# Two stacked decoder layers on one core: another order for loading the expert weights

## The chip, the cores and the metric

The kernel runs on one core of a Trainium2 chip. The metric is the device time of one execution in microseconds (us). A core has a matrix engine (TensorE, PE in the profile), a vector engine (VectorE, DVE), an activation engine (ScalarE, ACT) and a sync engine (SyncE, SP) which here issues nearly all DMA transfers. Each engine works through its own instructions in their order and waits on semaphores of the others.

## The reference

Two layers over 256 tokens of width 1024. Each has a norm, four mixers and their gates, an output projection, then a feed-forward part: dense in the first layer, and in the second the best two of eight experts for each token. The change touches only that expert part:

```python
def _moe(h, router_w, wg, wu, wd):
    logits = t @ router_w                       # (256, 8)
    vals, idx = lax.top_k(logits, 2); w = softmax(vals)
    gate = sum(one_hot(idx, 8) * w[..., None], axis=1)
    for e in range(8):
        y = y + gate[:, e:e+1] * ((silu(t @ wg[e]) * (t @ wu[e])) @ wd[e])
```

`wg[e]` and `wu[e]` are 1024 x 3584, `wd[e]` is 3584 x 1024, all float32: 44 MB for each expert, 352 MB in all, read once.

## The kernel before

The first 857 us of the execution are the first layer and the mixers of the second. After that comes `experts()`, in `run()`.

**Whole experts and pairs.** The experts are sorted by how many tokens they have. The four largest are *whole*: up to 128 tokens each. The four smallest make two *pairs*: two experts side by side, 64 tokens each. The hidden width 3584 is cut into 7 chunks of 512. A *step* is one chunk of a whole expert or of a pair. Of 42 steps 28 are whole and 14 are of pairs; `PAIRS` puts one pair step after every second whole step, and the last ones close together.

**Pieces.** The weights come in pieces of 1 MB (128 x 2048 float32). A whole step uses six: two for the gate product (`gps`), two for the up product (`ups`), and then two for the down product (`yps`) of the whole step before. A pair step uses twelve: first four for the down product of the pair step before (`yps`), then four for `gps`, four for `ups`. In each of a pair's products calls (L1308) two pieces, one for each expert, are used together. `pieces()` lists all 336 pieces in the order of use.

**Split pieces and raw pieces.** A whole expert's piece lands in a `raw` tile and is then split: ACT copies its high part into `wh` (L164), DVE subtracts that and leaves the low part in `wl` (L171), and PE makes three products of it (L196 to L198). Its raw tile is free once DVE is done. There are three `wh` and three `wl` buffers. A pair's piece lands in a `rawn` tile and PE reads it there (L1308); its tile is free once PE has used it.

**The ring.** `Stream.begin()` takes raw tiles in turn out of nine (`rawp` has 4, `rawx` 5). SP issues a transfer once the tile nine places earlier in the order of loading is free. All issues stand in one queue of SP. `Stream.get()` (called in `products()`) hands out the next piece, and before that writes the loading and splitting of pieces into the program until two beyond this one are there. PE, ACT and DVE keep the order in which the program is written.

**Other work in the steps.** Small jobs wait in a list `units`; `tick()` runs one between products. Before an expert's or a pair's first step its tokens are gathered (`gather()`: tile `dms` on DVE, then eight groups of products L1218 into `gaps`, copied out by ACT and DVE); after its last step the result is scattered (L1341). Gate products end in L1371 (`act`, on ACT). `turned()` transposes `act` of a step for its down product: PE L243, then ACT L1325 for a pair (`aT`), ACT L214 and DVE L215 for a whole expert (`ah`, `al`); it stands after the gate products of a whole step, for the pair and then for the whole step before.

Of the kernel before, what the change touches and what calls it, by code (L numbers as in the profile page):

```python
# [25 lines left out]
KD = D // P  # L26
# [10 lines left out]
NB = 4  # L37
# [27 lines left out]
def trunk(ctx: ExitStack, tc: tile.TileContext, x, pos, invf, rows, cols, wst, w_a, w_kvf, w_gate, w_br,  # L65
          w_out, f_g, f_u, f_d, router, e_g, e_u, e_d, gfin, out):
    nc = tc.nc
# [89 lines left out]
    def load_hi(src, n=512, parts=1, pool=None):  # L157

        raw = (pool or rawp).tile([P, 4 * n], F32, tag="raw", name="raw")
        hi = whp.tile([P, 4 * n], F32R, tag="wh", name="wh")  # L160
        sls = [slice(4 * n * i // parts, 4 * n * (i + 1) // parts) for i in range(parts)]
        for sl in sls:
            nc.sync.dma_start(raw[:, sl], src[:, sl])
            nc.scalar.activation(hi[:, sl], raw[:, sl], AF.Copy)  # L164
        return raw, hi, sls, n

    def load_lo(raw, hi, sls, n):

        lo = whp.tile([P, 4 * n], F32R, tag="wl", name="wl")
        for sl in sls:  # L170
            nc.vector.tensor_sub(lo[:, sl], raw[:, sl], hi[:, sl].bitcast(F32))  # L171
        return hi.rearrange("p (k n) -> p k n", k=4), lo.rearrange("p (k n) -> p k n", k=4)
# [874 lines left out]
    def experts(l, mine):  # L1047
# [3 lines left out]
        with ExitStack() as c2:  # L1051
# [10 lines left out]
            class Stream:  # L1062

                def __init__(self, srcs, ahead=2, whole=False):
                    self.srcs, self.begun, self.ready, self.ahead = list(srcs), [], [], ahead
                    self.whole = whole

                def begin(self):  # L1070
                    (w, q, *rest), parts = self.srcs.pop(0)
                    if q and not places:
                        _, vals = nc.values_load_multi_w_load_instructions(
                            idx_i[0:1, 0:NE], engines=[E.SP], min_val=0, max_val=NE - 1)
                        places.extend(vals)
                    src = w[(places[q] if q else 0, *rest)]
                    pool = ([rawp] * 4 + rawx)[turn[0] % (4 + NX)]
                    turn[0] += 1
                    if q < NB or self.whole:
                        self.begun.append(load_hi(src, parts=parts, pool=pool))  # L1080
                    else:
                        raw = pool.tile([P, 4 * W], F32, tag="raw", name="rawn")
                        n = 4 * W // parts
                        for i in range(parts):
                            nc.sync.dma_start(raw[:, i * n:i * n + n], src[:, i * n:i * n + n])
                        self.begun.append(raw.rearrange("p (k n) -> p k n", k=4))

                def fill(self):
                    while (self.srcs or self.begun) and len(self.ready) <= self.ahead:
                        if not self.begun:  # L1090
                            self.begin()
                        b = self.begun.pop(0)
                        self.ready.append(load_lo(*b) if isinstance(b, tuple) else b)

                def get(self):
                    self.fill()
                    return self.ready.pop(0)

            gate, mx, e8 = small("gate", NT, NE), small("mx", 2, NT), small("e8", NT, NE)
            gts = small("gts", NT, NE, 2, dtype=F32R)  # L1100
# [55 lines left out]
            class Expert:  # L1156
# [2 lines left out]

                def __init__(self, *at, base=0):  # L1160
                    self.at, self.pair, self.base = at, len(at) > 1, base
                    self.y = [None, None]

            def pieces(steps):

# [8 lines left out]
            def run(steps, groups, stream, tagx):  # L1174


                with ExitStack() as c3:
                    wk = c3.enter_context(tc.tile_pool(name=f"xk{tagx}", bufs=2, reuse_waits="tile"))
                    units, late = [], []

                    def tick(n=1):

                        for _ in range(n):
                            if late:
                                late.pop(0)()
                            if units:
                                then = units.pop(0)()
                                if then:
                                    late.append(then)
# [18 lines left out]
                    def token_tiles(group):  # L1208
                        for x in group:
                            if x.pair:  # L1210
                                x.tok = wk.tile([P, KD, P], F32, tag="xs", name="xs")
                            else:
                                x.tok = wk.tile([P, KD, 2, P], F32R, tag="xb", name="xb")
# [7 lines left out]

                    def gather_out(group, ps, part, k2):
                        for i, x in enumerate(group):
                            ks, src = slice(2 * k2, 2 * k2 + 2), ps[:, :, i * P:(i + 1) * P]
                            if not x.pair:
                                nc.scalar.activation(x.tok[:, ks, part], src, AF.Copy)
                            elif part == 0:
                                nc.scalar.activation(x.tok[:, ks], src, AF.Copy)
                            else:
                                nc.vector.tensor_add(x.tok[:, ks], x.tok[:, ks], src)  # L1230
# [45 lines left out]
                    def gather_now(x, dm):  # L1276


                        token_tiles([x])
                        banks = [(4 * g, part, py.tile([P, 4, P], F32, tag="y", name="gaps0"))  # L1280
                                 for g in range(2) for part in range(2)]
                        for t in range(NT):
                            if t:
                                mine.slot(psm, t)
                            for k0, part, ps in banks:
                                for i in range(4):
                                    k = k0 + i
                                    nc.tensor.matmul(ps[:, i], mine.parts[t][part][:, k * P:(k + 1) * P], dm[:, t, 0],
                                                     start=not t and not i, stop=t == NT - 1 and i == 3)
                                if t:  # L1290
                                    dst = x.tok[:, k0:k0 + 4, part]
                                    if part:
                                        nc.vector.tensor_copy(dst, ps)
                                    else:
                                        nc.scalar.activation(dst, ps, AF.Copy)
# [87 lines left out]
                    def turned(pair):  # L1383
                        if prev[pair] and not lhs[pair]:
                            lhs[pair] = act_T(prev[pair][0], prev[pair][2])
# [7 lines left out]
                    for n, (x, c) in enumerate(steps):  # L1393
                        if n == 0:
                            if x.base:
                                gather([x])
                                tick(len(units) + 1)
                            else:
                                gather_now(x, mine.dm)
                        if x.pair:  # L1400
                            down_of(1)
                            prev[1] = x, c, gate_up(x)
                            continue

                        def meanwhile():
                            if not x.base:
                                if n == 0:
                                    in_places()
                                if n == 1:
                                    gates()  # L1410
                                if n in groups:
                                    gather(groups[n])
                                if n == 0:
                                    units.append(lambda x=x: back([x], mine.dm))
                            for pair in (1, 0):
                                turned(pair)
                        a = gate_up(x, meanwhile)
                        down_of(0)
                        prev[0] = x, c, a


                    nc.scalar.activation(frs[:, 0:1], epsc, AF.Sqrt)
# [4 lines left out]
                    x = steps[-1][0]  # L1427
# [33 lines left out]
            q = [Expert(i) for i in range(NB)]  # L1461
            p = [Expert(i, i + 1) for i in range(NB, NE, 2)]
            steps = [(x, c) for x in q for c in range(NFC)]
            for at, s in reversed(list(zip(PAIRS, [(x, c) for x in p for c in range(NFC)]))):
                steps.insert(at + 1, s)
            groups = {steps.index((x, c)): g for x, c, g in
                      ((q[0], 0, [p[0], q[1]]), (q[1], 3, [p[1], q[2]]), (q[2], 3, [q[3]]))}
            order = [(s, 1) for s in pieces(steps)]
            order[-6:] = [(s, 4) for s, _ in order[-6:]]
            stream = Stream(order[3:])  # L1470
            stream.ready, stream.begun = mine.first[:1], mine.first[1:]
            run(steps, groups, stream, "a")
            finish("a")
            with tc.If(nc.values_load(over_i[0:1, NE:NE + 1], min_val=0, max_val=1) > 0):
                for i in range(NE):
                    with tc.If(nc.values_load(over_i[0:1, i:i + 1], min_val=0, max_val=1) > 0):
                        x = Expert(i, base=P if i < NB else P // 2)
# [80 lines left out]
```

## Time and profile before

| what | value |
|---|---|
| runs | 1753.75, 1751.87, 1753.71 us; median 1753.71 |
| the profiled execution | 1754.09 us, of which the span from the first to the last instruction is 1752.4 us |
| busy share of the span | PE 95%, weight loads of PE 70%, DVE 60%, ACT 47% |
| mean granted clock of TensorE | 0.985 |
| moved by DMA | 497.69 MB, mean 284 GB/s |
| chain of waits | PE 47%, DMA 8%, ACT 4%, DVE 4% |

Busy PE is not PE at its peak: the ends of its pipelined matmuls are modelled. In the rows below a `windows` row gives a stretch in us from the span's start, its length, the busy time of PE, PEld, DVE, ACT and POOL with instruction counts, the granted clock, the DMA engines' busy share and GB/s. A `timeline` row gives start, duration, engine, line, operation, out<-in, count, and in brackets the idle time before it with what ended it. A row of the chain of waits gives start, duration, and what it was spent on. In the name of a row's operand `in_e_g`, `in_e_u` and `in_e_d` are the gate, up and down weights of the experts.

### The profile page before, as it was taken

To read this page: it belongs to the slowest core of one execution; us is meant where nothing else is said; L and a number is where in the kernel's file an instruction comes from. 1 tells how busy PE (TensorE), PEld (TensorE's weight loads), DVE (VectorE), ACT (ScalarE), POOL (GpSimd) and SP (SyncE) were. 2 spreads that over 40 slices of the span, in tenths; PEclk is the share of its full clock that TensorE was granted. 3 is DMA by queue.
4 is the path that set the end of the run, shared out by engine and by line. 5 is a ranking of instruction groups with operands and counts; after the bars stand their busy time and mean duration, and the time that the engine had idled before them with its cause. 6 is when DMAs were issued, how large, how long until landed. Compare 5 with 4: busy or idle time off the path is not lost.

```text
span 1752.4 us, 20308 instructions
## 1 busy us (share of the span) xinstructions
PE 1672.5 (95%) x7800; PEld 1225.4 (70%) x7800; DVE 1052.6 (60%) x1284; ACT 828.0 (47%) x878; POOL 12.5 (1%) x28
## 2 busy tenths in 40 slices
PE   8999999999999999999889999999999899999995
PEld 6888888888887888888776557556556655755552
DVE  6779976555545678976665437435545633754434
ACT  6655454544434656444465426434443533543333
POOL 1000000000000000000000000000000000000000
PEclk9999999999999999999899999999999999999998
DMA  7444444555554543446568999999999989999994
GB/s 269 169 145 145 169 173 162 207 180 190 190 182 154 197 145 123 170 176 257 221 231 361 408 421 421 421 392 386 422 415 420 417 344 418 420 421 420 420 419 162
DMA packets 74362, 497.69 MB, mean 284 GB/s; under 512 B 8368, under 2 KB 8416, under 8 KB 15888
## 3 DMA queue, kind: packets, MB, share of 16 engines
q1 hardware_dynamic: 73008, 492.93, 71.5%
q0 software_dynamic: 960, 2.85, 0.6%
q8 instruction: 63, 1.03, 0.2%
q10 hardware_dynamic: 288, 0.52, 0.1%
q14 instruction: 43, 0.35, 0.1%
HBM read 495.22 MB, written 1.05 MB: 283 GB/s over the span
## 4 chain that ended last, share of the span: by engine, by line
PE 47%; DMA 8%; ACT 4%; DVE 4%; issue 1%; SPq 0%; ACTq 0%; DVEq 0%
DMA raw<-in_e_g 6%; PE yps L1308 6%; PE gps L197 3%; PE yps L197 3%; PE yps L196 3%; PE yps L198 3%; PE zps L196 3%; PE gps L198 3%; PE zps L198 3%; PE zps L197 3%; PE gps L196 3%; PE ups L196 3%; PE ups L197 3%; ACT wh L164 3%; PE ups L198 3%; DVE wl L171 3%
## 5 line engine op out<-in xcount | busy, mean ns | idle before, releaser
L171 DVE TENSOR_TENSOR wl<-raw,wh 128x2048 fp32r<-128x2048 f32 (+1 forms) x312 | 681.0, 2194 | 554.6 <-ACT wh L164 554.2
L164 ACT ACTIVATE wh<-raw 128x2048 fp32r<-128x2048 f32 (+1 forms) x312 | 571.1, 1838 | 348.0 <-PE zps L198 76.5
L196 PE MATMUL zps<-wh,hh 128*128 128x512 f32 (+1 forms) x544 | 215.9, 397 | 3.7 <-ACT wh L214 2.6
L197 PE MATMUL zps<-wl,hh 128*128 128x512 f32 (+1 forms) x544 | 210.0, 386 | 0.9 <-DVE wl L215 0.9
L198 PE MATMUL zps<-wh,hl 128*128 128x512 f32 (+1 forms) x544 | 209.8, 386 | 0.0
L1371 ACT ACTIVATE act<-gps 128x512 f32<-128x512 f32 x42 | 25.1, 598 | 289.1 <-PE gps L1308 249.3
L196 PEld LDWEIGHTS zps<-wh,hh 128*128 128x128 f32 x544 | 102.9, 189 | 24.7 <-ACT wh L214 3.0
L197 PEld LDWEIGHTS zps<-wl,hh 128*128 128x128 f32 x544 | 102.8, 189 | 21.4 <-DVE wl L215 2.5
L198 PEld LDWEIGHTS zps<-wh,hl 128*128 128x128 f32 x544 | 102.7, 189 | 20.7
L1308 PE MATMUL ups<-rawn,xs 128*64 128x512 f32 x448 | 102.8, 593 | 3.7 <-DMA rawn<-in_e_u 3.7
L197 PE MATMUL gps<-wl,xb 128*128 128x512 f32 x224 | 92.4, 413 | 11.9 <-DVE wl L171 11.9
L503 DVE SCALAR_TENSOR_TENSOR cacc<-ypad,col,cacc 128x256 f32<-128x256 f32 x240 | 101.3, 477 | 0.0
L1308 PE MATMUL yps<-rawn,aT 128*64 128x512 f32 x448 | 99.7, 596 | 0.0
L1308 PE MATMUL gps<-rawn,xs 128*64 128x512 f32 x448 | 98.6, 592 | 0.0
L196 PE MATMUL gps<-wh,xb 128*128 128x512 f32 x224 | 93.1, 416 | 3.4 <-ACT wh L164 3.4
L196 PE MATMUL yps<-wh,ah 128*128 128x512 f32 x224 | 88.9, 397 | 3.7 <-ACT ah L214 3.7
L196 PE MATMUL ups<-wh,xb 128*128 128x512 f32 x224 | 92.0, 411 | 0.0
L198 PE MATMUL gps<-wh,xb 128*128 128x512 f32 x224 | 90.8, 405 | 0.0
L197 PE MATMUL yps<-wl,ah 128*128 128x512 f32 x224 | 88.5, 395 | 1.6 <-DVE wl L171 1.6
L197 PE MATMUL ups<-wl,xb 128*128 128x512 f32 x224 | 89.0, 397 | 0.0
L198 PE MATMUL ups<-wh,xb 128*128 128x512 f32 x224 | 88.9, 397 | 0.0
L198 PE MATMUL yps<-wh,al 128*128 128x512 f32 x224 | 88.3, 394 | 0.0
(319 smaller groups left out, 2359.1 us busy)
## 6 DMA issues: line engine op xcount, KB each, us to landing
raw<-in_e_g SPq DMA_DIRECT2D x56, 1024.0 KB, 12.2
raw<-in_e_u SPq DMA_DIRECT2D x56, 1024.0 KB, 14.0
rawn<-in_e_g SPq DMA_DIRECT2D x56, 1024.0 KB, 12.9
rawn<-in_e_u SPq DMA_DIRECT2D x56, 1024.0 KB, 8.6
raw<-in_e_d SPq DMA_DIRECT2D x54, 1024.0 KB, 16.9
rawn<-in_e_d SPq DMA_DIRECT2D x52, 1024.0 KB, 16.3
raw<-in_w_gate SPq DMA_DIRECT2D x32, 1024.0 KB, 4.8
raw<-in_w_a SPq DMA_DIRECT2D x28, 1024.0 KB, 4.8
```

What stands on the lines that cost most here:

```text
L164: nc.scalar.activation(hi[:, sl], raw[:, sl], AF.Copy)
L171: nc.vector.tensor_sub(lo[:, sl], raw[:, sl], hi[:, sl].bitcast(F32))
L196: nc.tensor.matmul(ps, xh, wh, start=first, stop=False)
L197: nc.tensor.matmul(ps, xh, wl, start=False, stop=False)
L198: nc.tensor.matmul(ps, xl, wh, start=False, stop=last)
L503: nc.vector.scalar_tensor_tensor(cacc[:, b], src, wcol, cacc[:, b], op0=OP.mult, op1=OP.add)
L1308: nc.tensor.matmul(ps[js], lhs(k)[:, js], w[:, kk], start=k == 0, stop=k == ktot - 1)
L1371: nc.scalar.activation(a, gps, AF.Silu)
```

## The change

The order of loading is no longer the order of use. Every piece gets a key, its place in the order of use, and a piece that is split gets 3.5 less; pieces are loaded in the order of their keys. Where whole pieces follow pair pieces, the first three of them thus move between the last four of the pair's. `get()` loads up to two places beyond the piece that it hands out, in the new order, but holds back a piece that is to be split when three split ones are already there and the wanted one is ready. The first gather is put into `units` after the first step's products and no longer between its gate and up products, and the loop `while x.got < KD` finishes a gather before its first use.

```diff
+                def __init__(self, srcs, begun=(), ahead=2, lead=3.5, whole=False):
+                    self.srcs, self.begun, self.ahead = list(srcs), list(begun), ahead
+                    self.split = [whole or q[1] < NB for q, _ in self.srcs]
+                    order = range(len(self.srcs))
+                    self.order = sorted(order, key=lambda i: i - lead * self.split[i])
+                    self.at = {i: k for k, i in enumerate(self.order)}
...
                 def begin(self):
-                    (w, q, *rest), parts = self.srcs.pop(0)
+                    i = self.order[self.next]
+                    self.next += 1
...
-                    if q < NB or self.whole:
-                        self.begun.append(load_hi(src, parts=parts, pool=pool))
+                    if self.split[i]:
+                        self.ready[i] = load_lo(*load_hi(src, parts=parts, pool=pool))
...
                 def get(self):
-                    self.fill()
-                    return self.ready.pop(0)
+                    i = self.n
+                    self.n += 1
+                    while self.next < len(self.order) and self.next <= self.at[i] + self.ahead:
+
+                        full = sum(self.split[j] for j in self.ready) == 3
+                        if full and self.split[self.order[self.next]] and i in self.ready:
+                            break
+                        self.begin()
+                    return self.ready.pop(i)
...
+                        while x.got < KD:
+                            tick()
...
-                                if n in groups:
+                                if n in groups and n:
                                     gather(groups[n])
-                                if n == 0:
-                                    units.append(lambda x=x: back([x], mine.dm))
...
+                        if n == 0 and not x.base:
+                            gather(groups[n])
+                            units.append(lambda x=x: back([x], mine.dm))
```

SP's queue where the second pair step's weights end and the third step's first chunk of a whole expert begins, before. `rawn` are pair pieces, `raw` whole ones, numbers are tiles, and rows without a transfer are left out:

```order
L1085 DMA rawn_7461<-in_e_u 128x2048
...
L1085 DMA rawn_7463<-in_e_u 128x2048
...
L1085 DMA rawn_7476<-in_e_u 128x2048
...
L1085 DMA rawn_7478<-in_e_u 128x2048
L163 DMA raw_7488<-in_e_g 128x2048
L163 DMA raw_7494<-in_e_g 128x2048
L163 DMA raw_7510<-in_e_u 128x2048
L163 DMA raw_7528<-in_e_u 128x2048
L163 DMA raw_7565<-in_e_d 128x2048
```

And the same place now:

```order
L1095 DMA rawn_7461<-in_e_u 128x2048
L163 DMA raw_7463<-in_e_g 128x2048
...
L1095 DMA rawn_7480<-in_e_u 128x2048
L163 DMA raw_7482<-in_e_g 128x2048
...
L1095 DMA rawn_7488<-in_e_u 128x2048
L163 DMA raw_7498<-in_e_u 128x2048
...
L1095 DMA rawn_7504<-in_e_u 128x2048
L163 DMA raw_7559<-in_e_u 128x2048
L163 DMA raw_7577<-in_e_d 128x2048
```

The first three whole pieces stand one, two and three places earlier among the pair's last; the pair's last piece stands three places later. The fourth whole piece keeps its place.

ACT around the same place, from the end of the whole step before the pair step on, before. The second `act` is the pair's, the third that of the whole step behind it:

```order
L1371 ACTIVATE act<-gps 128x512
L214 ACTIVATE ah<-ps_t 128x512
L164 ACTIVATE wh<-raw 128x2048 x2
L1371 ACTIVATE act<-gps 128x512
L164 ACTIVATE wh<-raw 128x2048 x4
L1371 ACTIVATE act<-gps 128x512
L1325 ACTIVATE aT<-ps_t 128x512
L214 ACTIVATE ah<-ps_t 128x512
L164 ACTIVATE wh<-raw 128x2048 x6
```

And now:

```order
L1383 ACTIVATE act<-gps 128x512
L214 ACTIVATE ah<-ps_t 128x512
L164 ACTIVATE wh<-raw 128x2048 x3
L1383 ACTIVATE act<-gps 128x512
L164 ACTIVATE wh<-raw 128x2048 x2
L1383 ACTIVATE act<-gps 128x512
L1337 ACTIVATE aT<-ps_t 128x512
L214 ACTIVATE ah<-ps_t 128x512
L164 ACTIVATE wh<-raw 128x2048 x7
```

One of the four splits that followed the pair's `act` now precedes it, and the fourth has moved behind the next `act`, `aT` and `ah`.

DVE in the first step, from the places of the experts (`whereq`) to the gates (`lg`), before:

```order
L1114 TENSOR_REDUCE whereq<-tmp 128x16
L171 TENSOR_TENSOR wl<-raw,wh 128x2048
L1203 TENSOR_TENSOR dms<-slots,whereq 128x2x64 x2
L1203 TENSOR_TENSOR dms<-slots,whereq 128x2x128
L171 TENSOR_TENSOR wl<-raw,wh 128x2048
L1376 TENSOR_TENSOR act<-act,ups 128x512
L171 TENSOR_TENSOR wl<-raw,wh 128x2048 x2
L1136 TENSOR_SCALAR lg<-lg,rs 128x8 x2
```

And now:

```order
L1124 TENSOR_REDUCE whereq<-tmp 128x16
L171 TENSOR_TENSOR wl<-raw,wh 128x2048 x2
L1388 TENSOR_TENSOR act<-act,ups 128x512
L171 TENSOR_TENSOR wl<-raw,wh 128x2048
L1213 TENSOR_TENSOR dms<-slots,whereq 128x2x64 x2
L1213 TENSOR_TENSOR dms<-slots,whereq 128x2x128
L171 TENSOR_TENSOR wl<-raw,wh 128x2048
L1146 TENSOR_SCALAR lg<-lg,rs 128x8 x2
```

The three `dms`, on which the first gather's products wait, stand two splits and an `act` later.

## Rows read from the trace of the kernel before

**Rows 1.** The page: DMA busy share in 40 equal slices of the span.

```profile
DMA  7444444555554543446568999999999989999994
```

**Rows 2.** Windows, each from one pair step's start to the next one's; last, eleven together.

```profile
974.72:1029.79 55.07, 55.07 (x253) 34.96 (x252) 30.20 (x17) 25.94 (x18) 0.00 (x0) 1.00 1.00 411
1029.79:1091.65 61.86, 57.88 (x260) 36.41 (x259) 32.40 (x21) 27.09 (x20) 0.00 (x0) 1.00 1.01 421
...
1157.54:1220.96 63.42, 59.78 (x281) 38.09 (x281) 31.73 (x21) 28.52 (x28) 0.00 (x0) 1.00 0.97 400
...
1526.96:1589.17 62.21, 58.35 (x256) 37.30 (x255) 31.37 (x19) 26.16 (x18) 0.00 (x0) 0.97 1.01 420
1589.17:1645.32 56.15, 55.27 (x254) 34.95 (x253) 30.10 (x17) 25.94 (x18) 0.00 (x0) 1.00 1.01 421
1645.32:1690.64 45.32, 41.35 (x178) 22.40 (x177) 15.46 (x9) 13.42 (x10) 0.00 (x0) 0.96 1.01 420
974.72:1645.32 670.60, 637.14 (x2884) 405.75 (x2883) 349.94 (x223) 297.56 (x228) 0.00 (x0) 0.99 0.99 410
```

**Rows 3.** Timeline of SP: the `ups` pieces of the pair step at 1157.54.

```profile
1150.37 14.62 SPq L1085 DMA_DIRECT2D rawn<-in_e_u  x4
```

**Rows 4.** Tile `rawn`: SP's two issues in 1161 to 1162, and their landing.

```profile
L1085 SPq DMA_DIRECT2D rawn<-in_e_u x2: 333/333/333, 1161.2 to 1161.8; - x2
...
DMA to landing us min/median/max: 4.7/5.7/6.7
```

**Rows 5.** Timeline of PE: the pair step at 1589.17 and what follows.

```profile
1589.17 7.09 PE L1308 MATMUL yps<-rawn,aT 128*64 128x512 f32 x32
...
1609.92 0.50 PE L196 MATMUL gps<-wh,xb 128*128 128x512 f32 x1
...
1616.65 1.03 PE L243 MATMUL ps_t<-ident,act 128*128 128x128 f32 x8
1617.44 0.48 PE L196 MATMUL ups<-wh,xb 128*128 128x512 f32 x1
...
1622.97 0.39 PE L196 MATMUL yps<-wh,ah 128*128 128x512 f32 x1
...
1628.41 0.39 PE L196 MATMUL gps<-wh,xb 128*128 128x512 f32 x1
```

**Rows 6.** Timeline of PE: last products of the pair step at 1645.32.

```profile
1665.02 3.65 PE L1308 MATMUL ups<-rawn,xs 128*64 128x512 f32 x14 [1.31 <-DMA rawn<-in_e_u]
```

**Rows 7.** Timeline of ACT: third whole piece behind a pair step, three of eleven times.

```profile
995.77 1.92 ACT L164 ACTIVATE wh<-raw 128x2048 fp32r<-128x2048 f32 x1 [0.57 <-DMA raw<-in_e_u]
...
1056.85 1.92 ACT L164 ACTIVATE wh<-raw 128x2048 fp32r<-128x2048 f32 x1 [0.59 <-DMA raw<-in_e_u]
...
1612.00 1.92 ACT L164 ACTIVATE wh<-raw 128x2048 fp32r<-128x2048 f32 x1 [0.58 <-DMA raw<-in_e_u]
```

**Rows 8.** Timeline of ACT and DVE, after the gate products that end at 1616.65.

```profile
1617.28 0.60 ACT L1371 ACTIVATE act<-gps 128x512 f32<-128x512 f32 x1 [0.84 <-PE ps_t L243]
...
1618.73 3.73 ACT L164 ACTIVATE wh<-raw 128x2048 fp32r<-128x2048 f32 x2
...
1620.69 4.50 DVE L171 TENSOR_TENSOR wl<-raw,wh 128x2048 fp32r<-128x2048 f32 x2 [1.11 <-ACT wh L164]
```

**Rows 9.** Chain of waits: end of gate products at 1061.66, and near the end.

```profile
1061.66 0.87 PE ps_t L243 x8
...
1697.75 12.22 DMA rawn<-in_e_u
...
1715.95 1.28 ACT L1422
```

**Rows 10.** Timeline of DVE and PE: the first gather.

```profile
868.34 2.28 DVE L171 TENSOR_TENSOR wl<-raw,wh 128x2048 fp32r<-128x2048 f32 x1
870.54 0.82 DVE L1203 TENSOR_TENSOR dms<-slots,whereq 128x128 fp32r<-128x128 f32 x3
...
871.42 1.22 PE L1218 MATMUL gaps<-dms,hh 128*128 128x256 f32 x4 [4.14 <-DVE dms L1203]
```

More of the change, by code (lines that the diff above doesn't have):

```diff
@@ L1062, in experts @@
             class Stream:
-                def __init__(self, srcs, ahead=2, whole=False):
-                    self.srcs, self.begun, self.ready, self.ahead = list(srcs), [], [], ahead
-                    self.whole = whole
-                def begin(self):
-                    (w, q, *rest), parts = self.srcs.pop(0)
+                def __init__(self, srcs, begun=(), ahead=2, lead=3.5, whole=False):
[4 more added lines that the diff above has]
+                    self.at = {i: k for k, i in enumerate(self.order)}
+                    self.ready, self.next, self.n = {}, 0, 0
+                def begin(self):
+                    i = self.order[self.next]
+                    self.next += 1
+                    if self.begun:
+                        b = self.begun.pop(0)
+                        self.ready[i] = load_lo(*b) if len(b) > 2 else b
+                        return
+                    (w, q, *rest), parts = self.srcs[i]
                     if q and not places:
@@ L1083, in begin @@
                         n = 4 * W // parts
[L1084 to L1093, printed above, removed]
-                def get(self):
-                    self.fill()
-                    return self.ready.pop(0)
+                        for j in range(parts):
+                            nc.sync.dma_start(raw[:, j * n:j * n + n], src[:, j * n:j * n + n])
+                        self.ready[i] = raw.rearrange("p (k n) -> p k n", k=4)
+                def get(self):
+                    i = self.n
[6 more added lines that the diff above has]
+                    return self.ready.pop(i)
             gate, mx, e8 = small("gate", NT, NE), small("mx", 2, NT), small("e8", NT, NE)
@@ L1161, in __init__ @@
                     self.at, self.pair, self.base = at, len(at) > 1, base
-                    self.y = [None, None]
+                    self.y, self.got = [None, None], 0
             def pieces(steps):
@@ L1223, in gather_out @@
                         for i, x in enumerate(group):
+                            x.got += 1
                             ks, src = slice(2 * k2, 2 * k2 + 2), ps[:, :, i * P:(i + 1) * P]
@@ L1279, in gather_now @@
                         token_tiles([x])
+                        x.got = KD
                         banks = [(4 * g, part, py.tile([P, 4, P], F32, tag="y", name="gaps0"))
@@ L1469, in experts @@
             order[-6:] = [(s, 4) for s, _ in order[-6:]]
-            stream = Stream(order[3:])
-            stream.ready, stream.begun = mine.first[:1], mine.first[1:]
+            stream = Stream(order, mine.first)
             run(steps, groups, stream, "a")
```

## The prediction

> **What bounds the kernel now.** I read the slices of the page first. DMA is at 40 to 70% until slice 21 and then at 90% or more almost to the end [rows 1]: the expert part is the one that moves the most bytes for its time, and the change touches nothing else but one gather. So I cut that part into windows, each from the start of one pair step to the start of the next [rows 2]. A full window (two whole steps and a pair step, 24 pieces) takes 55 to 68 us, 61.0 on average (670.60 / 11). The most that DMA reaches is 421 GB/s, which is 1.0486 MB / 421 = 2.49 us for a piece, 59.8 us for 24. The eleven windows together run at 410 GB/s, so DMA leaves (421 - 410) / 421 x 670.6 = 17.5 us unused. PE is busy for 637.14 of 670.60 us and misses 33.5 us, about 3 us in a window; in the window at 1589.17 it is busy for 55.27 of 56.15 us. The two engines lie close: DMA wants 59.8 us for a window, PE 55 to 58. Whatever makes PE wait more than about 3 us for each pair moves the bound to PE.
>
> Then I looked at how pieces arrive. In the ring the issue of a piece follows the release of the piece nine places earlier. Four `ups` pieces of a pair are issued over 14.62 us [rows 3], in time with the products that free the tiles, not as fast as SP could; two such pieces land 4.7 and 6.7 us after their issue [rows 4]. A pair step itself is 12 pieces used in 1609.92 - 1589.17 = 20.75 us [rows 5], while DMA takes 30 us for as many. So during a pair step the pieces that have come ahead are used up, and the whole steps behind it refill the stock. Call the start of a pair step S. The pair's last piece has place 11 behind S, the next three, whole ones, places 12 to 14. The third of these is split as soon as it lands, which dates it: at S + 21.05 (995.77 - 974.72), S + 22.83 (1612.00 - 1589.17), and where things are late at S + 27.06 (1056.85 - 1029.79) [rows 7]. Of the eleven windows eight are of the first two kinds and three (1029.79, 1091.65, 1526.96) of the late one.
>
> **The change, part by part.** It takes no product, split or byte away, so its price is waits alone.
>
> *The pair's last piece.* In SP's queue three whole pieces now stand among the pair's last four, so the pair's last piece moves from place 11 to place 14. Place 14 is issued on the release of place 5, which is a pair piece in both orders, so it lands when the third whole piece lands today: 21.05 to 22.83 in the undisturbed windows. PE must have it for the last half of `ups`: at 1665.02, where the last piece was late by 1.31 us, 14 matmuls followed and the step closed 3.65 us after they began [rows 6]. I take a landing of S + 22.0, between the two rows, because a PE that is slower presses the queue less. The pair then ends at S + 22.0 + 3.65 = S + 25.65 instead of S + 20.75: +4.9 us.
>
> *The three whole pieces ahead of it.* They are split while the pair computes, on ACT and DVE, which are free there. Today the two pieces of the gate product take 1616.65 - 1609.92 = 6.73 us; one piece of products is (1628.41 - 1617.44) / 4 = 2.74 us [rows 5], so 6.73 - 5.48 = 1.25 us of waiting for splits goes. The gate product ends +3.65 us.
>
> *The fourth whole piece.* There are three pairs of split buffers, so the fourth split cannot start with the others, and on ACT it now stands behind the next `act`, `aT` and `ah`, where the fifth stands today. The fifth's split starts at 1618.73, DVE's at 1620.69, and PE starts on it at 1622.97 [rows 5, 8], which is 6.32 us behind the end of the gate product. PE will want the fourth after `ps_t` and one piece, 1617.44 - 1616.65 + 2.74 = 3.53 us behind it. A new wait of 2.8 us. Today the fourth is split before that point and costs nothing.
>
> Sum for an undisturbed window: 3.65 + 2.8 = 6.4 us. In some windows small products of a gather or scatter stand between gate and up product and cover a part of the 2.8; I take off 1.0 on average, which leaves 5.4, and 8 x 5.4 = 43. The window at 1589.17 would be 56.15 + 6.4 = 62.6, above DMA's 59.8: PE is the bound then and nothing gives the wait back. In the three late windows the gate product ends today at 1061.66 - 1029.79 = S + 31.9 [rows 9]; with a landing at 22.0 it ends at 22.0 + 3.65 + 5.48 = S + 31.1, and the fourth piece adds 2.8: +2.0 each, +6.
>
> *The rest.* The first window (at 923.43), in which the ring has just filled, gets +2; its bounds are 0 and 6.4. The last pair's weights land when they land today; 12.22 us of the closing chain are a wait for `rawn` [rows 9], while the last whole splits come earlier and free ACT for the closing work: -1.6, between 0 and -4.
>
> *The first gather.* PE waits 4.14 us for `dms` between gate and up product today [rows 10]. That wait goes. But the three `dms` now come two splits of 2.28 us and an `act` later, and whoever uses the gathered tokens first may wait anew. As the trace shows no such place, the bounds are -7 and +3; I take -3, nearest to the row.
>
> Total: 43 + 6 + 2 - 1.6 - 3 = +46.4. The profiled execution has 1754.1 us, 0.4 above the median of the runs: 1754.1 + 46.4 = 1800.5, so **1800**. With 22.83 for the landing and nothing taken off, 8 x 7.2 + 10 - 4.6 gives 1817; with 21.05 and no wait for the fourth piece, 8 x 2.7 - 5 + 2 - 4.6 gives 1768. This is the forecast's own range.
>
> **Rivals.**
>
> *Faster, by an evener DMA.* The three split buffers act as three more places in the ring: raw tiles of whole pieces come free during the pair step, which today happens only with pair pieces. DMA would then lose its 17.5 unused us, and with -3 of the gather the time is 1734. For it speaks that DMA is busier than PE in most windows of [rows 2], so that a wait of PE could be paid with DMA time that is short anyway. It decides if place 14 lands by S + 17, before the last half of `ups`. Against it: the earliest third whole piece lies at 21.05, and place 14 hangs on the same release as before. The Trainium skill ("Perfetto Trace Analysis", section Optimization Strategy) says to find the gaps on the engine that limits, see what they wait for, and make that start sooner; it also reads the same gap again and again as a sign of too few buffers. By it the splits' 1.25 us are the thing to move ahead and the change is right; by the rows the piece that is pushed back costs 4.9. Chance 0.09.
>
> *The fourth piece is hidden.* Landing at 21.05, and the fourth's split finds its place in time: 1768. The order on ACT speaks against, the 974.72 window for it. Chance 0.20.
>
> *The clock.* The granted clock is 0.97 and 0.96 in the windows at 1526.96 and 1645.32, whose pairs end late, and 1.00 in the others [rows 2]. A clock of 0.97 over 62.21 us is 1.9 us lost, spent at 1.2 instead of 2.4 GHz. If each new wait of 4.9 us brings one such fall, eight times 1.9 is 15: 1816. The Trainium skill ("TensorE: Matmul & The Clock Gate", section HAM oscillation — how this bites in real kernels) tells of just this, a wait for data in every turn of a loop after which the engine starts cold each time; the rows here agree in kind, and by them it costs a third of the wait. Chance 0.20.
>
> *No change to be seen.* Every other wait of PE's 33.5 us goes, as DMA is now ahead, and only the new one at its least stays: 637.1 + 11 x (21.05 + 3.65 - 20.75) = 680.6, +10.0 against 670.6; with -1.6 and -7 it is 1755.5. That the order would not change at all is out: SP's rows show it changed. Chance 0.06.
>
> **How the numbers follow.** 0.45 for the forecast, 0.20, 0.20, 0.06 and 0.09 for the others. About 0.2% (3.5 us) is what a measurement of this kernel tells from no change. Faster by more: 0.09; within: 0.06; slower: 0.85. The range leaves out the fast case and the one of no change and a little at the top: 1764 to 1829.
>
> **What will show it.** The pair's `ups` products, 7.0 us long today, stretch to about 12, with a wait for `rawn` in them. The first whole `gps` stands right behind the pair's end with no wait for `wl`. A wait for `wh` or `wl` of 2 to 3 us opens in the middle of each following `ups`. Windows get longer than 60 us with DMA below 410 GB/s. I am wrong if the pair's `ups` still takes 7 us or if the windows stay at 56 to 62 us; I am wrong in the size if the clock in these windows falls below 0.96, or if the fourth piece is ready when `ups` wants it.

## The result and the profile after

The changed kernel takes 1819.65 us (median of four runs, 1814.90 to 1822.46), the kernel before 1753.65: a ratio of 1.0376 with a 95% interval of 1.0350 to 1.0402. That is slower by 66 us, where +46 us, 1800, was forecast, inside a range of 1764 to 1829. The profiled execution is the shortest of the four, 1814.9 us, 60.8 more than the profiled execution before (1754.09).

Here are granted clock and DMA in the 40 slices of the page of the changed kernel, to be read beside [rows 1].

```profile
PEclk9999999999999999998999999999999999999998
DMA  7444544555544444555789998898998798999994
```

The late slices, 9 nearly throughout before, now hold 7s and 8s: DMA has holes. The windows of the changed kernel, cut as in [rows 2], from pair start to pair start. After the length stand PE, PEld, DVE, ACT and POOL busy, then the granted clock, DMA's busy share and GB/s.

```profile
857.00:918.00 61.00, 55.42 (x242) 44.66 (x241) 45.37 (x60) 34.58 (x34) 0.00 (x0) 0.92 0.69 256
918.00:971.78 53.78, 50.57 (x232) 34.65 (x231) 30.90 (x22) 26.71 (x21) 0.00 (x0) 1.00 0.93 384
971.78:1036.42 64.64, 59.94 (x253) 36.59 (x252) 30.54 (x17) 25.68 (x18) 0.00 (x0) 0.95 0.96 390
...
1640.06:1704.76 64.70, 59.95 (x253) 36.60 (x252) 30.53 (x17) 25.67 (x18) 0.00 (x0) 0.95 0.97 397
...
971.78:1704.76 732.98, 663.21 (x2883) 409.50 (x2882) 352.19 (x223) 294.49 (x228) 0.00 (x0) 0.97 0.93 379
1704.76:1813.10 108.34, 86.30 (x353) 39.78 (x352) 33.22 (x39) 28.49 (x39) 0.00 (x0) 0.90 0.70 276
```

The eleven windows take 732.98 instead of 670.60 us, +62.4; the first window +2.5 (53.78, 51.29 before); the stretch from 857 us to the first pair 61.00 instead of 66.43, -5.4; the closing stretch +1.3 (108.34, 107.1 before). The sum is 60.8. In the two windows at 971.78 and 1640.06, which answer to the shortest of [rows 2] (55.07 and 56.15), PE's clock is 0.95 now, and DMA moves 390 and 397 GB/s instead of 411 and 421. Over the eleven windows DMA no longer runs near the most it reaches: 379 GB/s, where it moved 410 before.

The pair step that answers to [rows 5], on SP and then on PE. First SP's issues:

```profile
1643.73 0.33 SPq L163 DMA_DIRECT2D raw<-in_e_g  x1
1644.31 0.33 SPq L1095 DMA_DIRECT2D rawn<-in_e_u  x1
1647.17 0.33 SPq L163 DMA_DIRECT2D raw<-in_e_g  x1
1647.74 0.33 SPq L1095 DMA_DIRECT2D rawn<-in_e_u  x1
1650.60 0.33 SPq L163 DMA_DIRECT2D raw<-in_e_u  x1
1651.18 0.33 SPq L1095 DMA_DIRECT2D rawn<-in_e_u  x1
1654.04 0.33 SPq L163 DMA_DIRECT2D raw<-in_e_u  x1
```

Two pieces follow each release, as before, but one of each two is now a whole one. The pair's last piece is the issue at 1651.18 = S + 11.1. PE's timeline of the same step and the whole step behind it:

```profile
1640.06 7.09 PE L1320 MATMUL yps<-rawn,aT 128*64 128x512 f32 x32
...
1653.84 4.45 PE L1320 MATMUL ups<-rawn,xs 128*64 128x512 f32 x18
1660.92 5.34 PE L1320 MATMUL ups<-rawn,xs 128*64 128x512 f32 x14 [2.63 <-DMA rawn<-in_e_u]
1666.19 0.50 PE L196 MATMUL gps<-wh,xb 128*128 128x512 f32 x1
...
1671.78 1.03 PE L243 MATMUL ps_t<-ident,act 128*128 128x128 f32 x8
1672.57 0.48 PE L196 MATMUL ups<-wh,xb 128*128 128x512 f32 x1
...
1675.84 0.49 PE L196 MATMUL ups<-wh,xb 128*128 128x512 f32 x1 [0.29 <-ACT wh L164]
1678.17 0.50 PE L197 MATMUL ups<-wl,xb 128*128 128x512 f32 x1 [1.83 <-DVE wl L171]
...
1679.39 0.63 PE L198 MATMUL ups<-wh,xb 128*128 128x512 f32 x1
...
1682.38 0.39 PE L196 MATMUL yps<-wh,ah 128*128 128x512 f32 x1
```

Three things are to be read here. The last 14 products start at S + 20.86 behind a wait for `rawn`, and the pair ends at S + 26.13 instead of S + 20.75. Those 14 take 5.34 us, where the same 14 took 3.65 in [rows 6], because the clock falls shortly after they begin:

```profile
1658.00:1661.00 3.00, 0.37 (x3) 0.08 (x4) 1.39 (x2) 1.91 (x1) 0.00 (x0) 1.00 1.02 426
1661.00:1664.00 3.00, 3.00 (x10) 0.94 (x12) 1.71 (x1) 0.00 (x0) 0.00 (x0) 0.65 1.01 421
```

The granted clock is 1.00 through the wait and 0.65 in the 3 us behind it; between 1662 and 1665 it is 0.50, the lower level of 1.2 GHz. The gate product behind the pair has no wait for a split. And in `ups`, three pieces on, PE waits 0.29 + 1.83 us for the fourth split; soon after that one product takes 0.63 us instead of 0.39. ACT and then DVE at that place, to be read beside [rows 8]:

```profile
1672.41 0.60 ACT L1383 ACTIVATE act<-gps 128x512 f32<-128x512 f32 x1 [12.03 <-PE ps_t L243]
1672.90 0.59 ACT L1337 ACTIVATE aT<-ps_t 128x512 f32<-128x512 f32 x1
1673.38 0.61 ACT L214 ACTIVATE ah<-ps_t 128x512 fp32r<-128x512 f32 x1
1673.86 5.52 ACT L164 ACTIVATE wh<-raw 128x2048 fp32r<-128x2048 f32 x3
...
1675.82 6.70 DVE L171 TENSOR_TENSOR wl<-raw,wh 128x2048 fp32r<-128x2048 f32 x3 [1.11 <-ACT wh L164]
```

ACT has idled for 12.03 us and splits the fourth piece only behind `act`, `aT` and `ah`, because the program has it in that order. Only the last 3 us or so of that idle time could have been used: the piece was issued at 1654.04 and took 9.3 us to land, and a split buffer comes free about 3 us behind the start of the gate product, as the run with that split moved ahead shows below (it starts 1646.34 - 1643.26 = 3.08 us behind it). These 3 us would have been enough: in that run PE has no wait for it. The groups of PE's products by line, of the changed kernel (out<-in, count, busy us, mean ns of one, idle time before them and what ended it), and the same three of before:

```profile
L1320 PE MATMUL ups<-rawn,xs 128*64 128x512 f32 x448 | 128.1, 667 | 40.6 <-DMA rawn<-in_e_u 40.6
L197 PE MATMUL ups<-wl,xb 128*128 128x512 f32 x224 | 92.9, 415 | 20.4 <-DVE wl L171 20.4
L197 PE MATMUL gps<-wl,xb 128*128 128x512 f32 x224 | 89.2, 398 | 0.5 <-DVE wl L171 0.5
```

```profile
L1308 PE MATMUL ups<-rawn,xs 128*64 128x512 f32 x448 | 102.8, 593 | 3.7 <-DMA rawn<-in_e_u 3.7
L197 PE MATMUL ups<-wl,xb 128*128 128x512 f32 x224 | 89.0, 397 | 0.0
L197 PE MATMUL gps<-wl,xb 128*128 128x512 f32 x224 | 92.4, 413 | 11.9 <-DVE wl L171 11.9
```

Waits for the pair's pieces grow by 37 us, those for the split in `ups` by 20, and those for `wl` in `gps` shrink by 11. Last, the mean granted clock, which was 0.985 over 1752.4 us before:

```profile
core 0: 1813.1 us, clock 0.977
```

The share of the span that is missing to a full clock is 0.023 x 1813.1 = 41.7 us after and 0.015 x 1752.4 = 26.3 before: as an estimate, 15.4 us of the 60.8 are the clock, and the 45.4 that are left are waits. The three lines above, 37 + 20 - 11 = 46, fit this. The spread of the four runs goes with the clock too: the two shortest have 0.977, the two longest, 1821.8 and 1822.46 us, have 0.972 and 0.973.

### The profile page after: what moved, and what is told of

It is laid out like the page before. It is cut to its first block, busy times and chain, and to the rows that moved or that the text cites. A ratio compares the mean times of both kernels' runs of the same rounds, so it can differ in the third digit from the quotient of the medians.

```text
span 1813.1 us, 20305 instructions
## 1 busy us (share of the span) xinstructions
PE 1699.5 (94%) x7800; PEld 1227.4 (68%) x7800; DVE 1055.2 (58%) x1284; ACT 824.5 (45%) x878; POOL 12.3 (1%) x28
## 4 chain that ended last, share of the span: by engine, by line
PE 50%; DMA 7%; DVE 4%; ACT 3%; issue 1%; SPq 0%; ACTq 0%; DVEq 0%
DMA rawn<-in_e_u 7%; PE yps L1320 5%; PE ups L1320 4%; PE gps L196 3%; DVE wl L171 3%; PE yps L197 3%; PE gps L197 3%; PE gps L198 3%; PE yps L198 3%; PE zps L196 3%; PE yps L196 3%; PE gps L1320 3%; PE zps L198 3%; PE zps L197 3%; PE ups L197 3%; PE ups L198 2%
## 5 line engine op out<-in xcount | busy, mean ns | idle before, releaser
L1320 PE MATMUL ups<-rawn,xs 128*64 128x512 f32 x448 | 128.1, 667 | 40.6 <-DMA rawn<-in_e_u 40.6
L1320 PEld LDWEIGHTS ups<-rawn,xs 128*64 128x64 f32 x448 | 38.4, 151 | 127.6 <-issue 71.2
L196 PEld LDWEIGHTS zps<-wh,hh 128*128 128x128 f32 x544 | 102.8, 189 | 24.7 <-ACT wh L214 3.0
L198 PEld LDWEIGHTS zps<-wh,hl 128*128 128x128 f32 x544 | 102.6, 189 | 20.8
L197 PE MATMUL ups<-wl,xb 128*128 128x512 f32 x224 | 92.9, 415 | 20.4 <-DVE wl L171 20.4
L196 PE MATMUL ups<-wh,xb 128*128 128x512 f32 x224 | 94.7, 423 | 1.7 <-ACT wh L164 1.7
L215 DVE TENSOR_TENSOR al<-ps_t,ah 128x512 fp32r<-128x512 f32 x42 | 28.4, 688 | 115.1 <-ACT ah L214 114.9
L198 PE MATMUL ups<-wh,xb 128*128 128x512 f32 x224 | 91.6, 409 | 0.0
L196 PE MATMUL gps<-wh,xb 128*128 128x512 f32 x224 | 91.0, 406 | 0.0
L198 PE MATMUL gps<-wh,xb 128*128 128x512 f32 x224 | 89.2, 398 | 0.0
## 6 DMA issues: line engine op xcount, KB each, us to landing
raw<-in_e_d SPq DMA_DIRECT2D x54, 1024.0 KB, 13.7
```

The lines of the kernel that those rows point to most:

```text
L196: nc.tensor.matmul(ps, xh, wh, start=first, stop=False)
L197: nc.tensor.matmul(ps, xh, wl, start=False, stop=False)
L198: nc.tensor.matmul(ps, xl, wh, start=False, stop=last)
L215: nc.vector.tensor_sub(lo, src, hi.bitcast(F32))
L1320: nc.tensor.matmul(ps[js], lhs(k)[:, js], w[:, kk], start=k == 0, stop=k == ktot - 1)
```

## Experiments

Theory A: the loss is made of two waits of PE in each window, for the pair's last piece (three places later in the queue) and for the fourth split (behind the next `act` on ACT); PE's slack, the time that it can lose in a window without the window getting longer because DMA is the bound, covers a part of each. (In the expectations of the first runs theory A names the pair's last piece first; both waits stand side by side from the third run on, and A' is the pair's last piece alone.) Theory B: the clock's falls in these waits are a part of the loss of their own. The rivals are named with the runs. The kernel before was timed beside each (1752.6 to 1753.5 us).

**The order of loading, by its lead.** The first three runs change one number, the last puts the gather back.

```diff
-                def __init__(self, srcs, begun=(), ahead=2, lead=3.5, whole=False):
+                def __init__(self, srcs, begun=(), ahead=2, lead=0, whole=False):
```

> The new kernel with the loading order of before (lead 0), so only the first gather stands later. Theory A (place of the pair's last piece, and with it PE's wait): the whole loss goes, and what is left is the stretch before the first pair, which the two traces show 5.4 us shorter (66.43 to 61.00 us): 1748 us. Rival C (the later gather, or the new way of handing out pieces, carries part of the loss): above 1757.

Measured: 1747.95 us, ratio 0.9968 (0.9955 to 0.9980). The whole loss goes with the order. What is left of the change, the later gather and the new way of handing out pieces, is worth 5.2 us against the 1753.13 timed beside it. Its stretch from 857 us to the first pair is 61.1 us long, its windows 61.3 us on average.

With `lead=1.5`:

> Lead 1.5 instead of 3.5: one whole piece stands before the pair's last piece, which comes at place 12 instead of 14. Theory A: it lands near S + 16, before PE's last half of ups (S + 17.3), so no wait and no fall of the clock, and the splits' 1.25 us a window go: 1740 to 1750. Rival D (whole and pair pieces mixed in the queue make DMA itself slower, which is why it shows 379 instead of 410 GB/s): a third or more of the loss stays, 1770 or above.

Measured: 1748.70 us, ratio 0.9976 (0.9966 to 0.9986). One whole piece is mixed among the pair's here, and DMA moves 408 GB/s in the windows: the mixing as such costs nothing at this lead. But one thing was not as expected: PE does wait for the pair's last piece, 14.0 us in all against 2.6 with lead 0. That the time stays the same (the 0.75 us between the two runs are within their spread) does not show such a wait to be free, since the waits for `wl` in `gps` shrink from 13.7 to 0.4 us at the same time: this is the trade that the change was made for, and at this lead it comes out even.

With `lead=2.5`:

> Lead 2.5: the pair's last piece at place 13. Theory A: it lands near S + 18.4, some 1.1 us late, and the fourth split still stands behind the next act, aT and ah: about +1 - 1.25 + 2 to 3.5 us a window, most of it above what DMA hides: 1760 to 1775. Rival D, or a price by the place alone: two thirds of the loss, 1792.

Measured: 1782.39 us, ratio 1.0166 (1.0138 to 1.0193), between the two expectations. Its wait for the pair's last piece is hardly longer than with 1.5; what it has beyond that is the fourth split's wait. The two groups of lead 2.5, by line:

```profile
L1320 PE MATMUL ups<-rawn,xs 128*64 128x512 f32 x448 | 117.4, 620 | 14.4 <-DMA rawn<-in_e_u 14.3
...
L197 PE MATMUL ups<-wl,xb 128*128 128x512 f32 x224 | 94.2, 421 | 20.3 <-DVE wl L171 20.3
```

I had the fourth split's wait at 2 to 3.5 us a window, most of it not hidden by DMA, but took off 1.25 for the splits that are won, which lead 1.5 has won already; the step from lead 1.5 to 2.5 costs 34 us, 3 us a window.

The gather where it was, with lead 3.5:

```diff
-                                if n in groups and n:
+                                if n in groups:
                                     gather(groups[n])
+                                if n == 0:
+                                    units.append(lambda x=x: back([x], mine.dm))
...
-                        if n == 0 and not x.base:
-                            gather(groups[n])
-                            units.append(lambda x=x: back([x], mine.dm))
```

> The new loading order with the first gather where it was. Theory A: the loss of the experts' windows stays and the 5.4 us won ahead of the first pair go: 1825. Rival C: clearly below 1815.

Measured: 1823.19 us, ratio 1.0409 (1.0390 to 1.0428). As expected of theory A, though against the spread of these runs the 3.5 us between it and the changed kernel are not a number by themselves. In its trace the first pair begins at 920.89, so the stretch from 857 us on is 63.9 us, between the 66.43 of before and the 61.00 of the changed kernel: by these single traces 2.9 of the 5.4 us are the gather's place. What the other 2.5 are, these runs don't separate.

**The fourth split.** `get()` counts its limit from the place of use where that is further:

```diff
-                    while self.next < len(self.order) and self.next <= self.at[i] + self.ahead:
+                    while self.next < len(self.order) and self.next <= max(self.at[i], i) + self.ahead:
```

> The new loading order (lead 3.5), but the limit of get() counts from the place of use where that is further, so the fourth whole piece is split ahead of the next act again. Theory A (two waits add up, the pair's last piece and the fourth split): the 20.4 us of PE's waits for wl in ups go, with the falls of the clock behind them, which lead 2.5 and lead 1.5 tell apart at 34 us together: 1786. Theory A' (the pair's last piece alone is the loss): 1815 or more.

> Lead 2.5 with the fourth split ahead of the next act. Lead 1.5 has the same 14 us of waits for the pair's last piece as lead 2.5 and yet no loss. Theory A: without the fourth split's wait lead 2.5 comes to 1746 to 1756. Theory A': it stays near 1782.

Measured: with lead 3.5 1781.87 us, ratio 1.0162 (1.0145 to 1.0180); with lead 2.5 1759.22, ratio 1.0036 (1.0024 to 1.0049). ACT with lead 3.5 now splits the fourth piece before `act`, and PE has no wait for it:

```profile
1646.34 1.92 ACT L164 ACTIVATE wh<-raw 128x2048 fp32r<-128x2048 f32 x1 [7.20 <-PE gps L198]
1649.51 0.60 ACT L1383 ACTIVATE act<-gps 128x512 f32<-128x512 f32 x1 [1.25 <-PE ps_t L243]
```

```profile
L1320 PE MATMUL ups<-rawn,xs 128*64 128x512 f32 x448 | 130.9, 676 | 43.9 <-DMA rawn<-in_e_u 43.9
```

The wait for the pair's last piece is as long as in the changed kernel (43.9, 40.6), and 38 us of the loss are gone. So the line that decides where the fourth split stands is worth more than half of the loss, on top of the other wait. Lead 2.5 comes out 3 us above its range: with 24.7 us it waits longer for the pair's pieces than the 14.3 I took over, probably because the whole steps are shorter and the ring has less of a lead.

The fourth split alone, in the loading order of before:

```diff
+                        j = self.order[self.next]
+                        if j > 3 and i < j - 1 and i in self.ready and self.split[j - 3:j + 1] == [True] * 4 \
+                                and not self.split[j - 4]:
+                            break
```

> The loading order of before (lead 0, gather later, as in the run at 1747.95 us), but the fourth whole piece behind a pair is split where the new kernel has it, behind the next act, aT and ah. The pair's last piece is not moved. Theory A with the slack that the kernel before has (6.6 us for 36 us of more products): a wait of 2 us with a fall of 1.6 us in each window is within PE's slack of some 3 us, so most is hidden: 1748 to 1760. Rival (each of the two waits costs its whole length wherever it stands): 1748 + 34 = 1782.

Measured: 1765.28 us, ratio 1.0063 (1.0045 to 1.0081), 17 us above lead 0, 5 above the expected range. PE waits as long for it as in the changed kernel, and has no wait for the pair at all:

```profile
L197 PE MATMUL ups<-wl,xb 128*128 128x512 f32 x224 | 93.8, 419 | 20.3 <-DVE wl L171 20.3
...
L1324 PE MATMUL ups<-rawn,xs 128*64 128x512 f32 x448 | 98.5, 592 | 0.0
```

Against lead 0 (1748): the fourth split alone +17, the pair's last piece alone +34, both +72. Together they cost 21 us more than apart. A part of this is the clock. The time missing to a full clock, on average over the runs of each kernel, is 24.8 us with lead 0, 30.4 with the fourth split alone, 31.6 with the pair's last piece alone and 45.9 with both: 9 us more than the two parts add up to, as an estimate. The other 12 fit a slack that each of them uses up, so that apart each loses a part of its length to time that PE had to wait for DMA anyway; no run shows these 12 by themselves.

**The slack and the clock.** In each pair step six matmuls of `ups`, three of the four parts of its first half for both experts, are computed twice, into the same place (`again` is set only there):

```diff
...
+                        for kk in range(3 if again else 0):
+                            for j, w in enumerate(ws):
+                                js = slice(j * n, j * n + n)
+                                nc.tensor.matmul(ps[js], lhs(kk)[:, js], w[:, kk], start=True, stop=True)
```

In the kernel before:

> The kernel before with the same six matmuls twice in each pair step: 14 x 2.6 = 36 us more for PE. If DMA is the bound in the windows (PE misses 33.5 us in eleven of them), most of it is hidden: 1753 to 1765. If PE is the bound, it costs all of it: 1790.

Measured: 1760.13 us, ratio 1.0044 (1.0030 to 1.0058). The 36 us of products cost 6.6. Not all that is saved is slack: the mean clock of its runs is 0.989, where the kernel before has 0.985, which is some 7 us. The eleven windows of that run:

```profile
976.88:1652.01 675.13, 657.98 (x3015) 410.88 (x3014) 350.25 (x223) 297.65 (x228) 0.00 (x0) 0.99 0.98 407
```

PE is busy for 20.8 us more than in [rows 2] and the windows are 4.5 us longer: DMA is the bound of the kernel before, and PE's slack in a window is of about the size that the prediction read.

In the changed kernel:

> The new kernel; of the up product of each pair step the first six matmuls of the first half are done twice (2.6 us, into the same place, which the product then starts anew), so PE works while the pair's last piece is on its way. Theory B (the wait of 2.6 us lets the clock fall, and the fall costs as much again): the 14 ups products, 128.1 us busy against 98.6 for the gps products of the same size, get short again: 1820 - 25 = 1795, although PE does 36 us more. Without B: 1820 to 1830.

Measured: 1803.87 us, ratio 1.0294 (1.0275 to 1.0313): 16 us faster with 36 us more of products. The pair step of that run, with the doubled products in L1316:

```profile
1640.63 7.04 PE L1324 MATMUL gps<-rawn,xs 128*64 128x512 f32 x32
1647.50 2.74 PE L1316 MATMUL ups<-rawn,xs 128*64 128x512 f32 x12
1650.07 8.12 PE L1324 MATMUL ups<-rawn,xs 128*64 128x512 f32 x32
```

```profile
core 0: 1799.5 us, clock 0.988
```

Most of the wait is filled (10.5 us are left of 40.6). No clock falls at the pair: wherever its last 14 products stand by themselves in this run's chain of waits, they take 3.65 us. The clock is 0.988 over the run, above that of the kernel before. 0.012 x 1799.5 = 21.6 us are missing to a full clock, 20.1 fewer than in the changed kernel; with 36 us of products more and 30 us of waits fewer that makes -14, near the -16 measured. The rest of what the expectation hoped for was miscounted: of the 29.5 us by which the `ups` products are longer than `gps`, half is only a wait that cuts the group in two and shows its modelled end twice (4.45 + 3.65 instead of 7.04 us).

Both edits:

> Both edits on the new loading order: the fourth split ahead of the next act, and the six matmuls done twice in each pair step. Apart they brought 38 us (1819.65 to 1781.87) and 16 us (to 1803.87). If the fourth split's wait and the fall of the clock at the pair's last piece are separate parts of the loss, they add up: 1766. If they share a part (the clock that falls at the fourth split is won once): 1770 to 1782. If with both PE is no longer the bound: 1748 to 1755.

Measured: 1776.15 us, ratio 1.0129 (1.0112 to 1.0146), 5.7 below the fourth split alone. They don't add up, and the time lies in the middle of what was expected if they share a part. The clock is 0.988 here too, but the fourth split's edit had it at 0.981 already: 0.019 x 1782.9 - 0.012 x 1774.3 = 12.6 us are won here, against 20.1 in the run before. That is 7.5 of the missing 10 us, as an estimate. The wait for the pair's last piece is 14.7 us behind the doubled products, where 10.5 are left without the fourth split's edit, which may be the rest.

## Why the prediction was right, and where it was not

The direction, the place and the mechanism held; the size was 20 us short. Cut at the pair's end and at the gate product's end, the average window was 21.3 + 8.0 + 31.6 us before and is 26.0 + 6.2 + 34.5 now. Point by point:

- *The pair's last piece.* Forecast: landing at S + 22.0, pair's end at S + 25.65. In the eleven windows it lands at S + 20.8 to 22.2, 21.3 on average, and the pair ends at S + 24.5 to 27.5, 26.1 on average. The landing was near the lower row, 21.05 [rows 7], probably because a PE that is the bound lets DMA come ahead as far as the ring allows. The end came later nonetheless, through the clock.
- *The splits ahead.* The gate product behind the pair has no wait for `wl` (0.5 us in all, 11.9 before), as forecast. It is 1.85 us shorter on average, where I had 1.25 in an undisturbed window.
- *The fourth split.* Forecast: 2.8 us, less 1.0 for what covers it. Measured in the clear window: 0.29 + 1.83 = 2.1 us, and 1.6 more, since eight products behind it run at the lower clock until 1682.38. From the gate product's end to the next pair, windows are 2.8 us longer on average; I had 2.1. The experiments show that this part alone decides 38 us of the loss when the other wait is there.
- *PE as the bound.* The windows are 66.6 us on average (732.98 / 11) with DMA at 379 GB/s, as forecast for the case that PE is slower than DMA's 59.8 us.
- *The first gather.* -5.4 instead of -3 for the whole stretch, of which the run with the old gather gives the gather's place 2.9. The wait of 4.14 us became one of 2.91 at the new place:

```profile
876.39 0.89 PE L1228 MATMUL gaps<-dms,hh 128*128 128x256 f32 x4 [2.91 <-DVE dms L1213]
```

- *First window and closing stretch.* +2.5 (forecast +2) and +1.3 (forecast -1.6). The last pairs pay the same wait as the others, which I had left out there.

The step that was mis-sized is the clock. I made it a rival, "the clock", with a price of 15 us for one fall at the pair in each of eight windows, and left it out of the sum. It came true, beside the forecast and not in its stead: 45.4 us of waits, where the sum had 46.4, plus 15.4 us of clock. That both numbers come out so near is luck in part. The gather and the closing stretch missed by -2.4 and +2.9, and the 15.4 are made of other falls than the rival had. By the chain of waits the last 14 products of the pair took more than 5 us in seven of the eleven windows and 3.65 in four:

```profile
1123.58 3.65 PE ups L1320 x14
...
1327.76 5.13 PE ups L1320 x14
```

And a second fall stands behind the fourth split in four of the eleven windows, those at 971.78, 1036.42, 1512.56 and 1640.06, which neither the forecast nor the rival had; against both stand falls of before that are gone with the waits of `gps`. My own sign of a wrong size, a clock below 0.96, showed in four windows, which have 0.95.

The reading behind that rival was wrong in two points. Before, the clock was not 1.00 in all windows but the two that I named: those at 1091.65 and 1220.96 have 0.97 as well, and the one at 1340.69 has 0.98. And where a pair ended late, the fall did not stand behind the pair's own wait. In the window at 1645.32 the 14 products behind the wait of 1.31 us take 3.65 us [rows 6], and the clock falls behind the next wait, for the gate product's split:

```profile
1671.83 0.50 PE L197 MATMUL gps<-wl,xb 128*128 128x512 f32 x1 [1.82 <-DVE wl L171]
...
1672.73 0.63 PE L197 MATMUL gps<-wl,xb 128*128 128x512 f32 x1
```

So the trace of before showed that a wait of PE for data can let the clock fall, but not that the pair's longer wait would. The rule of the Trainium skill that I weighed ("TensorE: Matmul & The Clock Gate", section HAM oscillation — how this bites in real kernels: a wait for data in each turn of a loop lets the engine start cold each time) agrees in kind with the rows of the changed kernel, at 1.7 us a fall, though in seven of eleven turns and not in each. A term for it belonged in the sum.

Of the other rivals, the evener DMA is out: DMA fell from 410 to 379 GB/s, and place 14 landed where the rows of before had it. The one of a hidden fourth piece is out in the changed kernel, but the run with that split moved ahead (1782 us, landing at S + 20.8 in its best windows) is nearly that case, priced at 1768 without the clock; its clock is 0.981. The one of no change failed because both waits were longer than what vanished.

The fastest version found is the one with the loading order of before and the later gather, 1747.95 us: 0.3% below the kernel before and 3.9% below the changed one. Lead 1.5, at 1748.70, can't be told from it.

## What to carry to other kernels

A transfer that is moved ahead in a full queue moves another one back, by as many places. So ask first which piece is late next and what stands behind it, before asking what the earlier piece saves: here the gate product won 1.85 us per window, and the pair lost 4.7, about 1 of them by the clock. Check too what else hangs on the place in the list: the limit of `get()` counted places of loading, and through that alone a fourth split slid behind three ACT instructions, though ACT had been idle just before them. Where two engines lie as close as here, what a wait costs depends on the slack that others leave and on whether the clock falls behind it, so effects measured apart did not add up.

## What was unexpected of the hardware

The granted clock fell to its lower level behind waits of PE of 2.6 us, and behind the fourth split's 0.29 + 1.83 us, and not every time: behind 2.63 us at 1660.92 the 14 products took 5.34 us, behind 2.69 us at 1533.48 they took 3.65.

```profile
1526.34 4.45 PE L1320 MATMUL ups<-rawn,xs 128*64 128x512 f32 x18
1533.48 3.65 PE L1320 MATMUL ups<-rawn,xs 128*64 128x512 f32 x14 [2.69 <-DMA rawn<-in_e_u]
```

Filling such a wait with products that are thrown away made the kernel 16 us faster. What decides in which windows the clock falls stays open.
